# A third listed order of the recorded operations on each engine, and a third listing of the places of the rotating buffers

## The chip, the cores and the metric

The kernel runs on one core of a Trainium2 chip. That core has a matrix engine (TensorE, PE in the rows), a vector engine (VectorE, DVE), a scalar engine (ScalarE, ACT), a general engine (GpSimd, POOL), and an engine that here only issues transfers (SyncE, SP; SPq is its DMA queue). They run their own instruction lists and wait for each other through semaphores. The metric is the device time of one launch in microseconds (us).

## The reference

One layer of a hybrid decoder for 1024 tokens of width 1024, in float32: sparse attention (8 heads of 64, three gated branches) beside a state-space mixer (S5), one input and one output projection.

```python
mod = jax.nn.silu(c) @ w_ada + b_ada
shift, scale, gate = jnp.split(mod, 3, axis=-1)
h = rms_norm(x, norm_g) * (1 + scale[:, None, :]) + shift[:, None, :]
proj = h @ w_in
q, kcr, vcr, ksl, vsl, kwn, vwn, z_a, g_br, u, z_s = jnp.split(proj, offs, axis=-1)
...
attn = nsa_attention(q, kc, vc, k_slc, kv_heads(vsl), k_win, kv_heads(vwn), gates)
attn = attn * jax.nn.silu(z_a)
y = s5_mixer(u, a_re, a_im, log_dt, b_re, b_im, c_re, c_im, d_skip)
y = jax.nn.gelu(y)
y = y * jax.nn.sigmoid(y @ glu_w.astype(jnp.float32) + glu_b.astype(jnp.float32))
ssm = y.astype(x.dtype) * jax.nn.silu(z_s)
mix = jnp.concatenate([attn, ssm], axis=-1) @ w_out
return x + gate[:, None, :] * mix
```

The compressed branch works on 63 blocks of keys, the selected branch on all 16 blocks of 64 keys up to the token (with 16 blocks in all every valid one is selected), the window branch on the last 512 keys.

## The kernel before

**Recording and issuing.** Nothing is issued where the code stands. Each `Recorder` puts an operation into the list of its job and engine; a job is a named piece of the layer. Then the text `ORD` is read from left to right: `ma3:s` issues the next operation of job `ma3` on SP, `u1m:p2` the next two of job `u1m` on PE (p PE, a ACT, v DVE, g POOL, s SP; x opens or closes a pool). `in_order` ties each engine to this order, so an engine executes its list strictly in a row: an instruction that waits holds up all that stand behind it on its engine. For SP that means that a transfer that waits holds up every later transfer. All instructions are issued by `issue`, so every row of the profile names line 375; the tiles tell them apart.

**Rotating buffers.** `SLOTS` gives for each kind of buffer the place that each allocation in turn takes: `w4` has 19 places of 4 KB for each partition, `w2` 13, `f2` 6, and `S`, `mm`, `pv` are places in PSUM. A new user of a place waits for the last reader of the one before it.

**The stages**, by the times of the profile:
- 0 to 33 us: the conditioning. `sc` is silu(c) broadcast over the partitions. Each `mod_chunk` loads 512 KB of w_ada (`wada`) and reduces it on DVE against `sc` into a column of `macc`: jobs `mb0` to `mb7` give the shift of the eight blocks of 128 features, `ma0` to `ma7` the scale, `mod0` to `mod7` the gate (needed at the output). `mc` makes the columns `gs` and `sh` of a block from them. x comes in two halves of four tiles; job `sq` squares and sums, `rstd` takes the inverse root, `xsc` scales the rows (DVE and ACT two tiles each), `xb` transposes by block and half on PE (`ptr`), `h` applies `gs` and `sh` on ACT into a high and a low part (`hhi`, `hlo`).
- 33 to about 280 us: the projections. A weight block `wraw` is split into `wh` and `wsp`; three 512-column matmuls for each block and half (high by high, high by low, low by high) give `ptp` (jobs `kva`, `kvb`, `qa`, `qb`) or `pcp` (`u`, `cz`/`z`, the compressed keys). In the same time the S5 parameters and its four scans: `xload` loads `s5X` from a DRAM copy `ud`, `scan` runs on DVE over the tiles `zw` and `z`, `prep` builds the tables of the next one on POOL and DVE (`ta`, `tb`, `s5CA`).
- about 300 to 655 us: attention, in the order of token blocks 0 to 3, then 7 to 4. Job `ha`*ih* computes the scores of block *i* and head *h* (`S`, PE) and reduces and exponentiates them (`st` on DVE, `pp` on ACT), `hb` and `hs` normalize, `hc` writes the fp16 pair `hl` and has SP load it transposed (DMA_TRANSPOSE `PT<-hl`), `ub`*ih* multiplies `PT` with the values (64-column matmuls `po<-V,PT`). `at`*i* loads the finished block back (`A<-ad`) and transposes it (`pat`), `ao` is its output projection. `z` pieces, `glu` (`pglu`) and the output projection (`po<-wo,oh`) fill PE between them.
- to 665 us: the last heads, `last_out`, `last_halves` and the stores.

Of the kernel before, what the change touches and what calls it, by code (L numbers as in the profile page):

```python
# [39 lines left out]
mb7:v xb11:p3 u3m:p2 h11:a u3m:p kva3:p mc5:v kva3:p s5p:v h11:a kva3:p s5p:v2 kva3:p s5p:v mc7:v kva3:p h40:a kva3:p3  # L40
# [266 lines left out]
    sm="012034143156747476471375146",  # L307
    vtmp="01",
    pos="01",
    S=(  # L310
        "0101100110100101011010010101010101001010010100101010101010101011010010101011010101010101010100101010"
        "1101"),
    w2s="01",
# [3 lines left out]
    b="0123313020",  # L317
    a="0122320300120312031320",
# [1627 lines left out]
```

## Time and profile before

| | |
|---|---|
| median of 3 runs | 666.67 us (665.85 to 672.79) |
| the profiled execution | 666.91 us |
| its span, first to last instruction | 665.1 us, so 1.8 us lie around it |
| mean granted clock of TensorE | 0.991 |
| PE busy | 611.2 us of the span |
| DVE busy | 565.0 us |
| ACT, POOL busy | 378.1 us, 150.6 us |

Busy time of an engine is the time in which it executed something. Matmuls overlap each other, so a busy PE is not necessarily at its best rate; the starts of matmuls that follow each other in a row tell that. An idle time has a releaser, the event after which the engine went on. A number in square brackets behind a row is such an idle time in us.

### The profile page before, as it was taken

The numbers are of one execution on the slowest core, as the hardware profiler recorded it, in microseconds if no ns is written. First come the engines' busy times: TensorE is split into PE (matmuls) and PEld (weight loads), VectorE is DVE, ScalarE is ACT, GpSimd is POOL, SyncE is SP. The second block draws the span as 40 slices with busy tenths as digits, with TensorE's granted clock in tenths as the row PEclk, the third lists the DMA queues.
The fourth block names the chain that finished last, engine by engine and source line by source line (L and its number), as shares of the span: only waits on it lengthen the run. The fifth ranks groups of instructions, "written<-read, shape, count | busy, mean of one in ns | idle before, by whom it ended". The sixth has DMA issues, their size and how long they took to land.

```text
span 665.1 us, 12579 instructions
## 1 busy us (share of the span) xinstructions
PE 611.2 (92%) x4662; PEld 493.3 (74%) x4662; DVE 565.0 (85%) x1107; ACT 378.1 (57%) x732; POOL 150.6 (23%) x162
## 2 busy tenths in 40 slices
PE   2198999999989999999989999899999989999986
PEld 0186888888778887878878777556787878788865
DVE  5999999899948799796777879889989979999864
ACT  2487433745335442446767686676775856766740
POOL 0134213604952012522120110213100213011010
PEclk9998999999989999999999999999999989999999
DMA  9984223425495642526449759999798899999987
GB/s 332 382 282 122 48 64 104 147 66 137 137 272 161 191 126 49 144 80 175 123 92 237 173 112 218 231 173 236 177 199 169 176 184 209 291 219 192 228 189 178
DMA packets 209759, 116.76 MB, mean 176 GB/s; under 512 B 159073, under 2 KB 188513, under 8 KB 209698
## 3 DMA queue, kind: packets, MB, share of 16 engines
q1 hardware_dynamic: 205858, 109.38, 67.4%
q0 software_dynamic: 3840, 6.57, 4.4%
q8 instruction: 37, 0.61, 0.4%
q14 instruction: 24, 0.20, 0.1%
HBM read 58.10 MB, written 18.61 MB: 115 GB/s over the span
## 4 chain that ended last, share of the span: by engine, by line
PE 37%; DMA 7%; DVE 4%; ACT 2%; issue 1%; SPq 1%; POOL 0%; POOLq 0%; ACTq 0%; DVEq 0%
PE po L375 16%; PE pcp L375 8%; PE S L375 8%; DMA PT<-hl 4%; PE pglu L375 2%; DVE st L375 1%; SPq L375 1%; DVE hl L375 1%; DMA za<-zad 1%; DMA wor<-in_w_out_dram 1%; ACT pp L375 1%; PE pqr L375 1%; ACT hl L375 1%; DMA xo<-in_x_dram 1%; PE pc L375 1%
## 5 line engine op out<-in xcount | busy, mean ns | idle before, releaser
L375 ACT ACTIVATE pp<-S,st 128x640 f32<-128x640 f32 (+7 forms) x128 | 89.0, 698 | 51.0 <-DVE st L375 33.7
L375 ACT ACTIVATE hl<-pp,st 128x640 f16<-128x640 f32 (+7 forms) x128 | 89.0, 730 | 32.5 <-DVE st L375 14.2
L375 DVE SCALAR_TENSOR_TENSOR hl<-pp,st,hl 128x640 f16<-128x640 f32 (+7 forms) x128 | 95.8, 776 | 11.6 <-ACT hl L375 11.5
L375 DVE TENSOR_REDUCE st<-S 128x1 f32<-128x640 f32 (+7 forms) x96 | 83.7, 884 | 13.0 <-PE S L375 12.5
L375 PE MATMUL pcp<-hhi,wh 128*128 128x512 f32 x208 | 84.1, 404 | 1.4 <-ACT G L375 1.1
L375 PE MATMUL po<-wo,oh 128*128 128x512 f32 x264 | 82.9, 399 | 1.7 <-DVE ps L375 0.8
L375 PE MATMUL ptp<-wsp,hhi 128*128 128x512 f32 x256 | 83.6, 407 | 0.0
L375 PE MATMUL pcp<-hhi,wl 128*128 128x512 f32 x208 | 82.3, 395 | 0.0
L375 PE MATMUL pcp<-hlo,wh 128*128 128x512 f32 x208 | 82.2, 395 | 0.0
L375 PE MATMUL po<-V,PT 128*128 128x64 f16 x1584 | 58.9, 194 | 6.4 <-DMA PT<-hl 6.3
L375 PE MATMUL S<-kT,qh 128*128 128x128 f32 (+3 forms) x192 | 61.3, 377 | 1.1 <-ACT pp L375 0.9
L375 PEld LDWEIGHTS <-PT 128*128 128x128 f16 x1584 | 54.1, 98 | 9.0 <-DMA PT<-hl 7.2
L375 PEld LDWEIGHTS po<-wo,oh 128*128 128x128 f32 x264 | 48.8, 188 | 14.0 <-ACT oh L375 1.3
L375 PEld LDWEIGHTS ptp<-wsp,hhi 128*128 128x128 f32 x256 | 48.2, 193 | 10.7 <-ACT V L375 0.2
L375 PE MATMUL S<-kT,ql 128*128 128x128 f32 (+3 forms) x192 | 54.2, 340 | 0.0
L375 PE MATMUL ptp<-wsp,hlo 128*128 128x512 f32 x128 | 51.6, 403 | 0.0
L375 PE MATMUL po<-wo,ol 128*128 128x512 f32 x120 | 47.4, 395 | 0.6 <-POOL ol L375 0.6
L375 PEld LDWEIGHTS pcp<-hhi,wh 128*128 128x128 f32 x208 | 39.2, 189 | 10.7 <-ACT G L375 1.5
L375 POOL TENSOR_TENSOR qr<-ropeb 128x512 f32<-128x512 f32 x16 | 23.5, 1489 | 102.2 <-DVE st L375 36.1
L375 PEld LDWEIGHTS pcp<-hlo,wh 128*128 128x128 f32 x208 | 39.1, 188 | 9.2 <-issue 0.2
L375 PEld LDWEIGHTS pcp<-hhi,wl 128*128 128x128 f32 x208 | 39.2, 188 | 8.1
L375 DVE SCALAR_TENSOR_TENSOR wada<-wada,sc 128x1024 f32<-128x1024 f32 x24 | 31.2, 1312 | 10.1 <-DMA wada<-in_w_adaT_dram 10.1
(310 smaller groups left out, 1291.0 us busy)
## 6 DMA issues: line engine op xcount, KB each, us to landing
wada<-in_w_adaT_dram SPq DMA_DIRECT2D x24, 512.0 KB, 7.8
wr<-in_w_in_dram SPq DMA_DIRECT2D x14, 512.0 KB, 4.3
x<-in_x_dram SPq DMA_DIRECT2D x8, 512.0 KB, 6.4
wor<-in_w_out_dram SPq DMA_DIRECT2D x8, 512.0 KB, 6.1
out_dram<-o SPq DMA_DIRECT2D x16, 256.0 KB, 2.7
wraw<-in_w_in_dram SPq DMA_DIRECT2D x15, 256.0 KB, 5.1
xo<-in_x_dram SPq DMA_DIRECT2D x14, 256.0 KB, 3.4
ud<-U SPq DMA_DIRECT2D x4, 512.0 KB, 2.8
```

The costliest lines, as they stand in the source:

```text
L375: op(*now(a), **{n: now(x) for n, x in k.items()})
```

## The change

Two tables are exchanged: `ORD`, the order of issue, and `SLOTS`, the places of the buffers. The jobs, their operations and the number of operations of each job on each engine stay the same (6602 operations in all), as do the flags `FLG` that choose engines, the code behind them and the sizes of the tables. The order differs nearly everywhere; the diff shows the first line of each table and the places below show the order that comes of it.

```diff
 ORD = """
-pre:v xl_1:s pre:s3 s5l:s lb:s s5l:s pre:s sc0:p pre:s2 ma3:s sq0:v mb1:s sc0:a s5p:v sc0:v ma1:s sq1:a s5p:v lb:s
-sc1:p s5p:v3 ma2:s s5p:v3 mb2:s s5p:v sq2:v sc1:a ma0:s sq4:a sc1:v ma5:s sq3:v mb3:s mb1:v xl_1:s ma3:v kvaw0:s xl_1:s
...
+prep0:g kvaw0:s xl_1:s s5l:s2 pre:s3 kvaw0:a pre:s2 kvaw0:g pre:s pre:v mb2:s s5p:v ma0:s sc0:p s5p:v2 lb:s s5p:v2 lb:s
+s5p:v4 sq0:v mb0:s sc0:a s5p:v sc0:v sq1:a ma1:s s5p:v sc1:p s5p:v2 sq4:a s5p:v5 sq2:v sc1:a sq3:v ma5:s kvaw1:s sc1:v
...
     w4=(
-        "0123425678098559AB83B5C2D97BCEF56AG79HE56I081CFCBBBD7HB32GAD8GC593BCD3C9C753A2BH7I958CIGA09DH7G3B7DH"
...
+        "012345674897972A0389A4BC289C7A5D4BE0FA98GB2421H3D494I095E184HGF7CC192IH94C5GI270FH70894FEGFE570H5H01"
...
```

In the order that the engines get, the waits for other engines' semaphores change in number: ACT 214 to 232, DVE 199 to 190, PE 92 to 95, POOL 90 to 93, SP 240 to 243 separate wait instructions.

**Place 1, DVE in the first 33 us.** `wada,macc<-wada,sc` is a chunk of the conditioning, `x_72<-x_72,rstd` the scaling of two tiles of the first half of x, `sh<-macc,bada` the column after which the first block can leave ACT, `sm` rows belong to the S5 parameters. Before (six more `sm` rows of the same two kinds are left out):

```order
L375 TENSOR_SCALAR x_72<-x_72,rstd 128x1024 x2
L375 TENSOR_TENSOR sm_170<-sm_170,sm_165 128x16
L375 TENSOR_SCALAR sm_170<-sm_170 128x16
...
L375 TENSOR_SCALAR gs<-macc,mod 128x1
L375 SCALAR_TENSOR_TENSOR wada,macc<-wada,sc 128x1024
L375 TENSOR_SCALAR sh<-macc,bada 128x1
```

Now:

```order
L375 SCALAR_TENSOR_TENSOR rsq<-rstd 128x4
L375 TENSOR_SCALAR gs<-macc,mod 128x1
L375 TENSOR_TENSOR rsq<-rsq,vtmp 128x4
L375 TENSOR_SCALAR gs<-macc,mod 128x1
L375 SCALAR_TENSOR_TENSOR rstd<-rsq,rstd 128x4
L375 TENSOR_TENSOR wsp<-wraw,wsp 128x512
L375 SCALAR_TENSOR_TENSOR wada,macc<-wada,sc 128x1024
L375 TENSOR_SCALAR x_72<-x_72,rstd 128x1024 x2
L375 TENSOR_SCALAR sh<-macc,bada 128x1
L375 SCALAR_TENSOR_TENSOR wada,macc<-wada,sc 128x1024 x2
L375 TENSOR_SCALAR gs<-macc,mod 128x1
L375 SCALAR_TENSOR_TENSOR wada,macc<-wada,sc 128x1024
```

The ninth chunk, which the first `sh` behind the scaling needs, stood behind the scaling and eight small `sm` rows; now the chunks that the first block needs are all ahead of it, six chunks stand ahead of the scaling instead of eight, one `wsp` row stands there in addition, and the `sm` rows have gone to the front of the list.

**Place 2, SP around the wait for the second scan.** All are loads: `wraw` a weight block of w_in, `w1s` and `w2s` weights of the compression, `wada` the chunks `mod`, `s5X` the input of a scan, `s5T` tables copied from `Kt`, `kTd` keys written out, `gq` a small gain, `dmask` a mask. Before; the second row (`wraw`) is the one that waits for the scan's `z`:

```order
L375 DMA gq_87<-in_gains_dram 64x1
L375 DMA wraw<-in_w_in_dram 128x512
L375 DMA w2s<-in_w_v_dram 128x2x64
L375 DMA wada<-in_w_adaT_dram 128x1024
L375 DMA w1s<-in_w_k_dram 128x2x256
L375 DMA wada<-in_w_adaT_dram 128x1024
L375 DMA s5X<-ud_100 16x8x128
L375 DMA wada<-in_w_adaT_dram 128x1024
L375 DMA s5X<-ud_101 16x8x128 x3
L375 DMA w1s<-in_w_k_dram 128x2x256 x3
L375 DMA s5X<-ud_100 16x8x128
L375 DMA w1s<-in_w_k_dram 128x2x256
```

Now; the second of the three `wada` rows is the one that waits for DVE:

```order
L375 DMA dmask<-in_dmask_dram 128x256
L375 DMA s5T<-Kt 16x8x16
L375 DMA w1s<-in_w_k_dram 128x2x256
L375 DMA wraw<-in_w_in_dram 128x512
L375 DMA s5X<-ud_100 16x8x128
L375 DMA wada<-in_w_adaT_dram 128x1024
L375 DMA s5X<-ud_100 16x8x128 x2
L375 DMA wada<-in_w_adaT_dram 128x1024
L375 DMA w1s<-in_w_k_dram 128x2x256
L375 DMA wada<-in_w_adaT_dram 128x1024
L375 DMA w1s<-in_w_k_dram 128x2x256
L375 DMA s5X<-ud_100 16x8x128
```

Before, the loads of this part stood in one piece behind the waiting row. Now three s5X rows, a `w1s`, a `wraw` and a `wada` of the rows shown stand ahead of the waiting one, and further on rows of `s5T` and `kTd`, which wait for other engines, are mixed in.

**Place 3, SP around the load of head 3 of block 3.** The numbers behind the names are those of the tiles: in the order before, `PT_4512` is the transposed load of that head; in the new one it is `PT_4571`. `zz` and `zad` rows move parts of the gate path, `ad` a finished block. Before:

```order
L375 DMA zz_4442<-zsd1_112 128x512
L375 DMA_TRANSPOSE PT_4446<-hl_4264 128x16x128
L375 DMA zz_4471<-zsd3_114 128x512
L375 DMA zad_110<-zz_4276 128x1024
L375 DMA_TRANSPOSE PT_4512<-hl_4302 128x16x128
L375 DMA_TRANSPOSE PT_4526<-hl_4448 128x16x128
L375 DMA zz_4554<-zsd0_111 128x512
L375 DMA_TRANSPOSE PTc_4637<-hlc_4622 128x8x128
L375 DMA_TRANSPOSE PT_4646<-hl_4358 128x16x128
```

Now:

```order
L375 DMA_TRANSPOSE PT_4422<-hl_4280 128x16x128
L375 DMA zz_4451<-zsd1_112 128x512
L375 DMA_TRANSPOSE PT_4455<-hl_4255 128x16x128
L375 DMA_TRANSPOSE PT_4474<-hl_4445 128x16x128
L375 DMA_TRANSPOSE PT_4515<-hl_4331 128x16x128
L375 DMA_TRANSPOSE PT_4555<-hl_4429 128x16x128
L375 DMA_TRANSPOSE PT_4571<-hl_4353 128x16x128
L375 DMA_TRANSPOSE PT_4594<-hl_4551 128x16x128
L375 DMA_TRANSPOSE PT_4622<-hl_4543 128x16x128
L375 DMA_TRANSPOSE PT_4644<-hl_4613 128x16x128
```

Nine of the ten rows shown are transposed loads now; before, plain transfers stood between them. Between the load of this head and the first PE row that reads it stand 39 PE rows before (1 `pglu`, 6 of 512 columns for scores, 15 `po` among them) and 113 now (13 `pglu`, 18 for scores, 63 `po`).

## Rows read from the trace of the kernel before

**Rows 1.** The page: the first line, the busy time of each engine and, in 40 equal slices of the span (16.6 us each), the GB/s that the DMA engines moved.

```profile
span 665.1 us, 12579 instructions
...
PE 611.2 (92%) x4662; PEld 493.3 (74%) x4662; DVE 565.0 (85%) x1107; ACT 378.1 (57%) x732; POOL 150.6 (23%) x162
...
GB/s 332 382 282 122 48 64 104 147 66 137 137 272 161 191 126 49 144 80 175 123 92 237 173 112 218 231 173 236 177 199 169 176 184 209 291 219 192 228 189 178
```

**Rows 2.** Busy time of each engine in six stretches: start and end, length, busy time and (instructions) of PE, weight loads, DVE, ACT, POOL, then the granted clock, the share of the DMA engines and GB/s.

```profile
0.00:33.30 33.30, 7.00 (x15) 3.11 (x16) 24.73 (x74) 12.78 (x20) 2.12 (x6) 1.00 0.96 356
33.30:182.90 149.60, 146.40 (x738) 119.98 (x738) 141.37 (x343) 77.96 (x126) 60.99 (x63) 0.99 0.43 123
182.90:199.50 16.60, 14.30 (x104) 12.57 (x103) 8.19 (x13) 5.33 (x10) 8.93 (x15) 0.90 1.00 272
199.50:415.70 216.20, 211.28 (x1434) 173.21 (x1434) 175.76 (x358) 124.92 (x305) 38.56 (x50) 1.00 0.57 145
415.70:648.40 232.70, 221.41 (x2218) 175.57 (x2217) 207.36 (x307) 155.56 (x268) 38.71 (x29) 0.99 1.00 205
648.40:665.10 16.70, 10.80 (x162) 8.85 (x160) 7.56 (x14) 1.56 (x5) 1.27 (x1) 0.93 0.75 178
```

**Rows 3.** What PE waited for in the whole span: tile that waited, releaser, us in total, times, longest.

```profile
PE ptr L375 <- DVE x L375: 16.5, 1, 16.5
PE po L375 <- DMA PT<-hl: 6.3, 5, 2.4
...
PE pkt L375 <- DVE kh L375: 2.3, 1, 2.3
PE pat L375 <- DMA A<-ad: 2.0, 1, 2.0
```

**Rows 4.** DVE in order of time, 10 to 31 us: start, duration, operation, output<-inputs, shapes.

```profile
14.55 1.23 DVE L375 SCALAR_TENSOR_TENSOR wada<-wada,sc 128x1024 f32<-128x1024 f32 x1 [0.84 <-DMA wada<-in_w_adaT_dram]
...
15.70 1.22 DVE L375 SCALAR_TENSOR_TENSOR wada<-wada,sc 128x1024 f32<-128x1024 f32 x1
...
25.60 2.31 DVE L375 TENSOR_SCALAR x<-x,rstd 128x1024 f32<-128x1024 f32 x2
27.83 0.16 DVE L375 TENSOR_TENSOR sm<-sm,sm 128x16 f32<-128x16 f32 x1
...
29.55 1.22 DVE L375 SCALAR_TENSOR_TENSOR wada<-wada,sc 128x1024 f32<-128x1024 f32 x1
...
30.80 0.21 DVE L375 TENSOR_SCALAR sh<-macc,bada 128x1 f32<-128x1 f32 x1
```

**Rows 5.** The same stretch on ACT and PE, each in order of time (PE from 27 us).

```profile
31.11 0.78 ACT L375 ACTIVATE hhi<-ptr,sh,gs 128x512 fp32r<-128x512 f32 x1 [1.25 <-DVE vtmp L375]
...
27.30 2.20 PE L375 MATMUL ptr<-ident,x 128*128 128x128 f32 x8 [16.54 <-DVE x L375]
...
33.38 1.20 PE L375 MATMUL ptp<-wsp,hhi 128*128 128x512 f32 x2
```

**Rows 6.** Busy time in a part of the projections, columns as in rows 2.

```profile
99.70:166.20 66.50, 66.50 (x376) 55.26 (x376) 61.66 (x114) 34.27 (x54) 25.91 (x23) 1.00 0.39 113
```

**Rows 7.** The stretch around 190 us: what SP's queue waited for longest there, and the first load after that wait; DVE and PE, each in order of time; and the granted clock in the last piece of it.

```profile
SPq L375 <- DVE z L375: 12.8, 1, 12.8
...
182.65 0.33 SPq L375 DMA_DIRECT2D wraw<-in_w_in_dram  x1
...
176.43 3.25 DVE L375 TENSOR_TENSOR z<-z 64x512 f32<-64x512 f32 x2
179.72 2.90 DVE L375 TENSOR_TENSOR z<-z,zw 64x512 f32<-64x512 f32 x2
...
191.49 1.23 DVE L375 SCALAR_TENSOR_TENSOR wada<-wada,sc 128x1024 f32<-128x1024 f32 x1 [3.89 <-DMA wada<-in_w_adaT_dram]
...
191.45 1.50 PE L375 MATMUL ph<-G,w1s 128*128 128x128 f32 x12
195.25 1.11 PE L375 MATMUL pkt<-ident,kr 128*128 128x128 f32 x4 [2.30 <-DVE kh L375]
196.16 4.11 PE L375 MATMUL ph<-G,w1s 128*128 128x128 f32 x24
...
195.50:199.50 4.00, 4.00 (x23) 3.92 (x23) 3.55 (x6) 1.89 (x4) 0.00 (x0) 0.61 1.08 276
```

**Rows 8.** The z tiles of the scans on DVE (durations in ns, least, median and most), and POOL's tensor operations with kr, by group: count, busy us, mean ns of one, idle before.

```profile
L375 DVE TENSOR_TENSOR z<-z,zw x12: 684/690/1436, 138.8 to 270.5; 64x512 f32<-64x512 f32 x8, 128x512 f32<-128x512 f32 x4
...
L375 POOL TENSOR_TENSOR kr<-ropeb 128x512 f32<-128x512 f32 x8 | 13.6, 1709 | 46.3 <-DVE ropeb L375 46.3
```

**Rows 9.** Transposed loads: the landing times of all 120 of them, and the three longest waits of PE for one, each in PE's order of time.

```profile
DMA to landing us min/median/max: 2.3/3.9/8.6
...
346.38 0.35 PE L375 MATMUL po<-V,PT 128*128 128x64 f16 x6 [1.59 <-DMA PT<-hl]
...
431.65 0.58 PE L375 MATMUL po<-V,PT 128*128 128x64 f16 x14 [2.38 <-DMA PT<-hl]
...
539.70 1.10 PE L375 MATMUL po<-V,PT 128*128 128x64 f16 x21 [1.93 <-DMA PT<-hl]
```

**Rows 10.** The end, on PE in order of time: its wait for A, and the last rows of the last head's scores.

```profile
633.50 0.63 PE L375 MATMUL pat<-ident,A 128*128 128x128 f32 x4 [2.00 <-DMA A<-ad]
...
634.66 0.29 PE L375 MATMUL S<-dmask,identb 128*128 128x128 bf16 x2
```

More of the change, by code (lines that the diff above doesn't have):

```diff
@@ new lines @@
+so1:v so2:g ha76:p4 ub71:p so5:a ub71:p7 ha76:v ub71:p4 ub73:p5 qt61:a ub73:p4 ha60:p4 hc75:v hb75:a ha60:p ct7:s
+so2:p2 hb74:a so2:p2 so1:v so2:p ha76:a so2:p hc74:v so2:p2 so4:a so2:p2 hs77:v hc75:v hc75:s so2:p2 ha61:p2 hs77:v
+at0:a qt61:v ha61:p3 at0:g ha61:p ub71:p8 ha61:v ub71:p so0:s ub71:p3 ub73:p2 hb77:a ub73:p3 ub36:p3 ub73:p6 ub70:p6
+ub71:p so2:v ub71:p5 ub37:p3 ub73:p6 ub74:p2 hb76:a ub74:p3 ha60:v ub74:p hc74:s ub72:p6 ca6:p4 ha61:a hc77:v ca6:p
+so2:p3 hb76:a so2:p2 hc76:v hc75:s so2:p ha60:a so2:p4 ca6:v so2:p hc76:s so2:p hc76:v ha60:p5 ca6:v so2:v ha60:p
@@ new lines @@
+ha63:p4 ha60:v ha63:p hc77:s ub71:p6 ha60:a ub72:p ha63:v ub72:p5 ub73:p6 ub72:p3 ub74:p6 ub72:p6 hb77:a ub75:p2
+ub35:p3 ub73:p2 ca6:v ub73:p4 ub72:p6 ub34:p3 ub74:p4 ha63:a ub74:p2 ub75:p2 so0:v ub75:p4 ub73:p4 ub75:p5 hc76:s
+ub75:p ub74:p6 hs61:v ha62:p2 so4:v ha62:p3 hs61:v so4:p hb61:a so4:p ha62:v so4:s so4:p3 ca6:a so4:p2 hc61:v hb61:a
+so4:p4 hc77:v so4:p ha62:a hc61:s ca5:p4 hc61:v ha62:p3 ca5:a ha62:p2 ca6:v ha62:p ub72:p4 hc61:s ub72:p2 ub74:p6
+ub72:p ha62:v ub72:p5 ub76:p12 ub77:p6 ha64:p3 ha62:a ha64:p hc77:s ha64:p ca5:p hb60:a ca5:p ha64:v ca5:p3 ha63:p2
@@ L306 @@
[L306 to L318 removed]
+        "0111234156743869242966132578AB4AC611C79C13860513C048B5018B006BC40173A85610BA7C30B4689A82319507C6B94A"
@@ new lines @@
+    sm="012034453463111616134714536",
+    pv="00010101010100011001000111001010000010111111100000000001101000101010100010",
+    vtmp="01",
+    S=(
+        "0101101011001011010101010101010100110100101010110010101010101010101010101010101101001010101010110110"
+        "1010"),
+    mm=(
+        "0100101010101010101000110110010110010010011000101010111010010100101011010010101010010011001010101001"
+        "01011100101"),
+    w2s="01",
+    b="0122331022",
+    a="0123331021123012031230",
+    pos="01",
@@ L319 @@
     pbh="01",
     mc="01010101",
-    lc="01010101",
-    st="01210310210231023102310231023102",
-    f2="01234053533140005243145120301452313450130242023230213534052134",
+    lc="01001010",
+    st="01230123013201320132031023102310",
+    f2="01230345241232045034230543150452401425134053435453102503425130",
     p4="01231320")
```

513 lines of the change are left out of this document (249 added, 264 removed).

## The prediction

> **What bounds the kernel now.** I read the busy times of the page first [rows 1]. Matmuls fill PE for 611.2 of 665.1 us and DVE is busy for 565.0, so no third engine can set the time for long; what a new order can change is the time in which PE stands. The profiled execution took 666.91 us, 1.8 more than its span and 0.24 more than the median of the three runs, so the sum below is made against 666.91 and needs no correction for the median. Then the stages [rows 2] say where each engine has room. In the first 33.3 us PE does next to nothing (7.00 us) and DVE 24.73: this stage is a chain through DVE. From 33.3 to 182.9 PE is full (146.40 of 149.60) but DVE is busy for 141.37, so both engines hold the stage. From 182.9 to 199.5 DVE falls to 8.19 of 16.60. From 415.7 to 648.4 PE is busy for 221.41 and DVE for 207.36 of 232.70, with the DMA engines at a share of 1.00. Third, the list of PE's waits [rows 3]: 16.5 us until x is scaled at the start, 6.3 us in five waits for transposed loads, 2.3 for the keys `kh`, 2.0 for a load of A. These four are the places where an order can save something by moving one row, and I take the change at each of them, plus the stage in which DVE is the other bound. A tally of the listed order beside the measured starts shows that before the two run within half a microsecond of each other on every engine, so distances in the list can be read as time.
>
> **Start, -3.6 us.** PE's first projection matmul starts at 33.38, 2.27 after `hhi` starts on ACT at 31.11, which waited for `sh` on DVE at 30.80 [rows 4, 5]. So DVE's list up to `sh` is the path. Its chunks run back to back from 14.55 at 1.15 us each (15.70 less 14.55), and at 27.83 the `sm` rows begin that last until 29.55, when the ninth chunk starts. In the new list three chunks fewer stand ahead of `sh` (six instead of eight ahead of the scaling, none instead of one behind): 3 x 1.15 = 3.45. The `sm` rows, 29.55 - 27.83 = 1.7 less the short `gs` row that stays, count 1.5; they go to the front, where DVE waits for x anyway (their cost if that cover were missing is the same 1.5). One `wsp` row is added, about half a chunk of the same kind of row with half the columns, 0.6. One weight block of 0.25 MB is loaded ahead of x; at the 332 GB/s of the first slice [rows 1] that delays the first chunk by 0.75. Sum: -3.45 - 1.5 + 0.6 + 0.75 = -3.6. The bounds: -1.9 if DVE waits for two of the six chunks as it does for the first at 14.55 (0.84 each), and -5.9 if two of the six don't hold the scaling (2 x 1.15), because they land while DVE is at x.
>
> **33 to 183 us, +2.0.** An earlier start of PE meets a DVE that has 61.66 us of work in the 66.5 us from 99.7 on, while PE has no gap at all [rows 6]. I summed the durations of the rows of both lists up to equal amounts of PE work: between 100 and 150 us of PE work the new list asks DVE for 47 to 49 us of work where the old one asks for 42 to 43. The 5 us more stand against 4.8 us of DVE idle in the rows; not all of it can be used, since rows wait for each other. I put the loss at 2.0, nearer to full use of the idle time because the same tally has DVE's work 1 to 3 us lower from 5 to 50 and from 150 to 200. Bounds 0 and +5.0.
>
> **The stall at 190 us, -2.0.** SP waits 12.8 us for the scan's `z` and issues the next load at 182.65; then all loads of that piece come at once, DVE waits 3.89 for one of them until 191.49, PE waits 2.30 for `kh` until 195.25, and the granted clock of the next 4 us is 0.61 [rows 7]: TensorE is at its lower level, 1.2 instead of 2.4 GHz, for most of that piece, after standing still. Twelve `ph` matmuls took 1.50 before the gap and 24 took 4.11 behind it, 1.1 more than twice 1.50. So 2.3 + 1.1 = 3.4 can be had. In the new list loads of this group stand ahead of the wait and others are spread behind it; but rows of `s5T` and `kTd`, which wait for other engines, stand among them, and whatever is behind them on SP waits too. I take somewhat more than half, -2.0, with bounds 0 and -3.4.
> The same wait has a second side. Two 64-partition `z` rows took 3.25 us and two more 2.90 [rows 7], 1.4 to 1.6 each, where the median of such a row is 0.69 [rows 8]; POOL runs its table rows beside them. The new list has POOL's `kr` rows (1.71 each, [rows 8]) beside this scan and its table rows a little later, so I expect no less overlap and give it no term.
> The Trainium skill, page "SBUF — State Buffer", says in the part on its two physically separate sides that the port pair which VectorE and GpSimd share is an exclusive lock, and the loser blocks for the whole instruction of the other. The long `z` rows agree with it in kind; by that rule the scan would be as slow beside `kr` as beside the table rows, SP's wait would stay 12.8 us long, and this term would be 0 instead of -2.0, the sum 663.3.
>
> **Transposed loads, -2.0.** In the old list the load of head 3 of block 3 has 39 PE rows between it and its first reader, which add up to 4.87 us; PE waited 2.38 for it at 431.65 [rows 9]. Now it has 113 rows and 18.3 us. The wait of 1.59 at 346.38 also loses its cause (3.58 to 9.21 us in the list); the one of 1.93 at 539.70 doesn't (5.03 to 4.45). Over all heads the median distance grows from 7.14 to 8.69, against landing times of 3.9 in the median and 8.6 at most. 2.38 + 1.59 = 4.0 can go. But nine such loads now stand almost in one piece on SP, and in that stage DVE and the DMA engines have little room [rows 2], so I count half: -2.0. Bounds 0, and -4.4 (6.3 less 1.93) if every wait except the last named goes.
> The Trainium skill, page "DMA: Bandwidth & Descriptors", section "Latency and other measured facts", gives 261 GB/s for a transposed load with a split middle dimension; 512 KB at that rate are 2.0 us, an estimate. By it 4.87 us would have been enough ahead of time, nothing would be gained by the move, and the sum would be 663.3; the trace differs, its least landing time is 2.3 and the median 3.9, so here the row decides.
>
> **The end, 0.** The load of A for block 5 cost 2.00 at 633.50 [rows 10]. In the new list it has 3.63 us of PE work ahead of its reader instead of 4.15, but is the second instead of the fifth transfer behind the head that it needs: no change. The last head's scores end at 634.95 [rows 10], 30.2 before the end of the span. They stand 18.0 us of PE work before the end of the list now, 22.4 before. If the chain behind them (reduce, exponent, `hl`, transposed load, `ub`, stores) can't be compressed, that is +4.4; in the old order PE was busy with other rows nearly all the time, so the chain has room and I take 0. Bounds -2.0 and +4.4.
>
> **Sum:** 666.91 - 3.6 + 2.0 - 2.0 - 2.0 + 0 = 661.3. All lower ends give 651.2 (-15.7), all upper ends 674.4 (+7.5).
>
> **Rivals.**
> *A, DVE takes the lead back.* If DVE holds the pace until 415 us, the 3.6 of the start return as waits of PE on DVE, and the stall is only moved: 666.91 - 2.0 = 664.9. For it: 94% busy DVE up to 183 [rows 2]. Against: its 16.6 us at half load from 182.9 on, in which a late DVE could catch up.
> *B, slower: attention tiles are held too long.* In the new list the last `ub` rows of head 7 of block 0 stand at 330 us of PE work instead of 300, those of heads 37 and 70 (block, head) at 425 instead of 404. Their `PT` tiles keep a place of the 19 in `w4` that much longer. If the next user of one such place is a load that SP reaches earlier, SP stands, and every transposed load behind it. A hold of 21 us longer, less the median distance of 8.7 that covers it, is 12.3 late for PE: with the start's gain 666.91 - 3.6 + 12.3 = 675.6. It decides from a hold that outlasts the cover by 10.4 us (3.6 + 6.8); below that the time stays within 1%.
> *C, all the waits go:* start -5.9, stall -3.4, loads -4.4, DVE 0: 653.2. For it: the four places are one row each, and DVE has 100 us of idle time in the whole span.
> *D, nothing changes on balance:* each engine's order does differ, but the gains at these places come back as waits elsewhere: 666.9.
>
> **Numbers.** What a measurement of this kernel can tell from no change is about 1%, here 660.0 to 673.3. Forecast 0.40, its own range 657.5 to 664.5, half of it under 660.0; C 0.20; A 0.18; D 0.10; B 0.12. Faster by over 1%: 0.20 + 0.20 = 0.40. Within: 0.20 + 0.18 + 0.10 = 0.48. Slower: 0.12. The range that leaves out the further half of C and most of B is 652 to 670.
>
> **What would show it.** The first `ptp` matmul at 29.8 (27.5 to 31.5); no DVE idle of over 2 us and no clock under 0.9 between 180 and 200; the sum of PE's waits for `PT` under 4.5 instead of 6.3, none over 1 us at block 3 head 3; PE idle between 100 and 166 us (by the old count) of 1 to 3 us with DVE as releaser; a load wait at A of about 2. Rival A would show as PE waits for DVE between 60 and 180 us that sum to the gain of the start, B as one long wait of SP's queue for PE between 350 and 480 with PE idle behind it. I would be wrong if the many waits of under 1 us, which the order changes everywhere and for which I have no term, sum to more than these places.

## The result, and the profile after

The changed kernel took 639.95 us in the median of four runs (637.93 to 643.35), the kernel before 667.28 beside it: a ratio of 0.958, 95% interval 0.951 to 0.965. That is 27 us faster where 5.6 were forecast, and outside the range of 652 to 670. The two profiled executions took 666.91 and 643.35 us, with spans of 665.1 and 640.3; what follows compares the spans, 24.8 us apart. (The profiled execution of after is the longest of its four.)

The page of after: its first line, busy times, and the granted clock in 40 slices.

```profile
span 640.3 us, 12597 instructions
...
PE 604.2 (94%) x4662; PEld 488.4 (76%) x4662; DVE 560.2 (87%) x1107; ACT 377.6 (59%) x732; POOL 143.1 (22%) x162
...
PEclk9999999999999999999999999999999999999999
```

Against [rows 1], PE's idle time fell from 53.9 us (665.1 - 611.2) to 36.1, which is 17.8 of the 24.8. The other 7.0 are in PE's busy time: the same 4662 matmuls were busy for 604.2 instead of 611.2. The mean granted clock rose from 0.991 to 1.000. Behind three waits of before (2.15 us at 61.67, 2.30 at 195.25, 1.93 at 539.70) PE's rows ran at the lower level for a while, as in [rows 7]; by the distances between their starts this cost 1.6, 1.7 and 1.6 us, some 5 of the 7.0. So a wait can be paid twice, and the waits alone don't give the sum. It need not be: one run of the old order (the second try at the start, in experiment 4) waited as long for the same row, 2.14 at 63.16, and its clock did not fall. PE was busy for 609.3 us in that run at a mean clock of 0.998, so the clock isn't all of the difference, and the remaining 2 us of the 7.0 have no cause here. Before, and then that run (columns as in [rows 2]):

```profile
62.00:66.00 4.00, 4.00 (x14) 3.22 (x12) 3.76 (x13) 4.00 (x7) 2.16 (x3) 0.57 0.37 124
```

```profile
63.00:67.00 4.00, 3.84 (x19) 3.21 (x20) 3.69 (x15) 4.00 (x8) 1.66 (x2) 1.00 0.46 138
```

What PE waited for, as in [rows 3] (tile, releaser, us in total, times, longest):

```profile
PE ptr L375 <- DVE x L375: 12.3, 1, 12.3
PE pcb L375 <- DVE sm L375: 5.7, 1, 5.7
PE S L375 <- ACT pp L375: 2.4, 4, 0.8
PE pcb L375 <- DVE sc L375: 1.9, 1, 1.9
PE po L375 <- DVE ps L375: 1.5, 1, 1.5
...
PE po L375 <- DMA PT<-hl: 0.9, 2, 0.5
...
PE ptr L375 <- ACT hf L375: 0.7, 1, 0.7
```

The transposed loads cost 0.9 instead of 6.3; the waits for `kh` and `A` are gone; the one for `hf` is 0.7. In before it was the third longest of the list, and [rows 3] leave it out:

```profile
PE ptr L375 <- ACT hf L375: 5.3, 2, 3.1
```

Once the projections run, no wait of PE is longer than 1.5 us.

The start, rows of DVE, ACT and PE, each in order of time (answering [rows 4, 5]):

```profile
14.22 1.22 DVE L375 SCALAR_TENSOR_TENSOR wada<-wada,sc 128x1024 f32<-128x1024 f32 x1
...
23.30 1.41 DVE L375 TENSOR_SCALAR x<-x,rstd 128x1024 f32<-128x1024 f32 x2
24.62 0.20 DVE L375 TENSOR_SCALAR sh<-macc,bada 128x1 f32<-128x1 f32 x1
```

```profile
24.46 1.06 ACT L375 ACTIVATE sq<-x 128x1024 f32<-128x1024 f32 x1 [0.55 <-DMA x<-in_x_dram]
25.43 0.19 ACT L375 ACTIVATION_READ_ACCUMULATOR sq<-x 128x1 f32 x1
25.52 0.76 ACT L375 ACTIVATE hhi<-ptr,sh,gs 128x512 fp32r<-128x512 f32 x1
```

```profile
24.10 2.21 PE L375 MATMUL ptr<-ident,x 128*128 128x128 f32 x8 [12.29 <-DVE x L375]
27.00 1.12 PE L375 MATMUL ptr<-ident,x 128*128 128x128 f32 x4 [0.70 <-ACT hf L375]
27.77 1.20 PE L375 MATMUL ptp<-wsp,hhi 128*128 128x512 f32 x2
```

`sh` starts 6.18 earlier (24.62 against 30.80), `ptp` 5.61 (27.77 against 33.38): 0.6 went to ACT, where `hhi` stood behind an `sq` row.

Busy time by stage, columns as in [rows 2] (PE, weight loads, DVE, ACT, POOL, clock, DMA share, GB/s):

```profile
27.70:170.00 142.30, 142.30 (x720) 116.73 (x720) 128.75 (x344) 79.21 (x131) 46.04 (x49) 1.00 0.49 141
170.00:196.00 26.00, 24.81 (x177) 21.73 (x176) 22.01 (x32) 7.14 (x13) 20.36 (x30) 1.00 0.74 207
```

PE has no gap from its first projection to 170 us, and the clock holds through the stretch where it was 0.61 before [rows 7].

**Where the time went.** To compare stretches of two orders I counted PE's work: each matmul stands for the usual distance from its start to the next one's for its kind, and the table gives the time at which so much work had been started. All kernels but after and before are experiments (below); "measured places" are a new listing for the same order.

```
us of PE work:                6     31    106    156    231    306    331    406    506    581
before                     34.7   65.3  142.3  199.6  278.2  363.0  389.0  472.4  586.3  659.6
after                      29.1   55.9  132.8  185.5  262.7  345.2  372.3  452.9  563.7  634.8
new start, then old        29.1   55.2  135.7  190.7  269.6  355.3  381.8  465.0  576.7  650.2
new two thirds, then old   28.5   55.6  132.4  184.7  261.6  343.7  376.8  459.1  572.3  645.2
old two thirds, then new   34.6   65.1  142.0  196.9  276.7  362.5  389.1  468.6  579.0  649.8
old order, measured places 35.1   64.6  142.8  196.9  273.2  355.4  381.7  461.5  575.1  647.1
new order, measured places 28.6   56.0  132.8  184.4  261.5  343.4  369.3  447.4  565.6  635.6
```

After leads by 5.6 us at 6 us of work, 9.4 at 31, 9.5 at 106, 14.1 at 156, 17.8 at 306 and 24.8 at the end. Some 70% of it is there half way through, and from 31 to 106, where both engines are full, nothing of it is lost. By the size of the loss (a matmul's start later than its usual distance): losses of over 1 us fell from 19.0 us at 11 places to 5.0 at 4; those of 0.3 to 1 us stayed (8.8, 9.1); those of 0.1 to 0.3 fell from 10.8 to 5.5.

### The profile page after: what moved, and what is told of

It reads as the page before. It is cut to its first block, busy times and chain, and to the rows that moved or that the text cites. A ratio compares the mean times of both kernels' runs of the same rounds, so it can differ in the third digit from the quotient of the medians.

```text
span 640.3 us, 12597 instructions
## 1 busy us (share of the span) xinstructions
PE 604.2 (94%) x4662; PEld 488.4 (76%) x4662; DVE 560.2 (87%) x1107; ACT 377.6 (59%) x732; POOL 143.1 (22%) x162
## 4 chain that ended last, share of the span: by engine, by line
PE 26%; DVE 11%; DMA 10%; issue 4%; ACT 3%; POOL 1%; SPq 0%; ACTq 0%; DVEq 0%; POOLq 0%
PE po L375 12%; PE S L375 6%; DMA PT<-hl 6%; PE pcp L375 5%; DVE hl L375 4%; DVE st L375 3%; DVE ps L375 1%; ACT pp L375 1%; DMA wor<-in_w_out_dram 1%; ACT hl L375 1%; DMA wr<-in_w_in_dram 1%; DMA yd<-Y 1%; DMA zz<-zsd 1%; PE pc L375 1%; POOL qr L375 1%
## 5 line engine op out<-in xcount | busy, mean ns | idle before, releaser
L375 ACT ACTIVATE hl<-pp,st 128x640 f16<-128x640 f32 (+7 forms) x128 | 90.0, 732 | 28.8 <-DVE st L375 13.1
L375 DVE SCALAR_TENSOR_TENSOR hl<-pp,st,hl 128x640 f16<-128x640 f32 (+7 forms) x128 | 97.6, 783 | 5.1 <-ACT hl L375 4.8
L375 POOL TENSOR_TENSOR qr<-ropeb 128x512 f32<-128x512 f32 x16 | 21.8, 1381 | 96.3 <-DVE ropeb L375 56.1
L375 PEld LDWEIGHTS S<-kT,qh 128*128 128x128 f32 x192 | 33.2, 190 | 8.1 <-ACT pp L375 3.0
```

The costliest lines, as they stand in the source:

```text
L375: op(*now(a), **{n: now(x) for n, x in k.items()})
```

## The experiments

Three questions are open, and the expectations name their theories by them. Does an early lead survive, or does DVE take it back behind the stretch that made it? Are the waits single rows, which a single move can take away, or does each stretch go as its whole list goes? And how much is the order, how much the listing of places? A mixed kernel takes the first entries of one list (an entry is one operation of a job) and then the rest in the other's order. Its places are a question of their own, since each listing belongs to one order.

**1. Mixed orders that keep both listings.** The places of both parts were renamed so that each allocation has its own listing's place, with 4, 6 and 0 of them changed at the joint. The last tokens ahead of the joint and the first behind it:

```diff
 ORD = """
-pre:v xl_1:s pre:s3 s5l:s lb:s
+prep0:g kvaw0:s xl_1:s s5l:s2 pre:s3 kvaw0:a pre:s2 kvaw0:g
...
+u1:p s5p:v2 u1:p s5p:v kvb3:p s5p:v cmpv:s pre:g hidk:s cKC:s
```

> The new order up to 50 us of PE work, the old one behind it, with both listings of places kept: those of the old one are renamed at the joint, so that only 4 allocations take another place. If a lead is kept: 9.5 less than before, 657. If the DVE work that the new start has put off (5.5 us) has to be paid in the full stage behind the joint: 660 to 663. If the lead is taken back: 665.

New order for 579 entries (about 50 us of PE work), then the old: **657.63 us, ratio 0.982 (0.977 to 0.987).** The lead is 10.1 at 31 us of work, 6.6 at 106, and 8.9, 8.6, 7.2, 9.4 at 156, 231, 331 and 581. Of the 3.5 lost up to 106, 0.9 go at the joint (a wait of 0.71 at 78.76), and 2.5 some 30 us later, in full stretch, where PE meets rows of POOL and DVE that come too late for it:

```profile
109.76 0.66 PE L389 MATMUL pkt<-ident,kr 128*128 128x128 f32 x4 [0.91 <-POOL kr L389]
...
111.12 0.26 PE L389 MATMUL pk<-s5c,BD 128*48 128x16 f32 x2 [0.29 <-POOL BD L389]
...
113.54 0.66 PE L389 MATMUL pkt<-ident,kr 128*128 128x128 f32 x4 [0.81 <-DVE kh L389]
```

Neither before nor after has a wait of PE between 31 and 106 us of work. So the old list takes a quarter of the lead back there. The 2.3 that return up to 156 are the stall at 190 us, which was shorter in this run; behind it the old order neither takes the lead back nor adds to it. Its rest shows the old waits in the old places, earlier by the lead ([rows 9, 10] had 2.38 at 431.65 and 2.00 at 633.50). PE, waits in order of time:

```profile
425.12 0.58 PE L389 MATMUL po<-V,PT 128*128 128x64 f16 x14 [2.54 <-DMA PT<-hl]
...
624.85 0.63 PE L389 MATMUL pat<-ident,A 128*128 128x128 f32 x4 [2.61 <-DMA A<-ad]
```

> The same joint at 304 us of PE work (342.7 us of time in the new kernel, 360.5 in the old): new order up to there, old one behind, 6 allocations on another place. If the stages add up and the listings are what broke the earlier mixed kernels: 17.8 less than before, 649. If attention in the old order does not bear an earlier start: over 655.

New order up to about 304 us of PE work (2934 entries; joint at `z5_5:p z5_3:p ub00:p3`): **655.21, ratio 0.979 (0.973 to 0.984).** It follows after to 306 (19.3 ahead of before), loses 7 just behind the joint in two waits for `PT` (2.14 at 348.06, 1.34 at 355.19) and what they delay, and goes like the old order from there.

> The counterpart at 322 us of PE work (379.5 us of time): old order up to there, new one behind, every allocation on the place that its listing gives, renamed. If the stages add up: 24.8 - 18.1 = 6.7 less than before, 660. If the new second half is quick only behind the new first half: 665 or more.

Old order for 3194 entries, then the new: **657.68, ratio 0.981 (0.976 to 0.987).** At 331 us of work it is level with before (389.1 against 389.0), and behind it gains 9.8, without the waits at block 3 head 3, at block 6 head 4 and at A. (On the way it was 2.7 ahead at 156, since its stall at 190 us was shorter: the wait for `kh` was 1.61, with no fall of the clock behind it. That much one execution differs from another at this place.) So the new front, with its listing, is worth some 17 to 19 us and the new last part, with its listing, some 7 to 10. The gain is spread over the program.

**2. Places alone.** The order is kept, and `SLOTS` is written anew by a rule. "Plain": the free place whose last reader stands furthest back in the list. "Measured": the place whose last reader ended first by the trace of that order. The first characters of `w4` (old order, measured rule):

```diff
     w4=(
-        "0123425678098559AB83B5C2D97BCEF56AG79HE56I081CFCBBBD7HB32GAD8G
+        "0123456789ABCDEFGHI2609BD31578ACHE09FG631I8CH7A27D57D920G5EB72
```

> The new order whole, but its listing of buffer places replaced by a plain rule: each allocation takes the place whose last reader stands furthest back in the list. If the order alone makes the gain: within 0.5% of the new kernel, 638 to 643. If the listing of places matters: over 645.

New order, plain places: **663.89, ratio 0.994 (0.991 to 0.998)**: 24 us of the 27 are lost by places alone. By after's measured times 37 of its allocations fall due before their place is released, by 51.8 us in all. It runs like after up to 156 us of work, then come waits such as these on PE, which after doesn't have:

```profile
208.43 6.21 PE L391 MATMUL ph<-G,w1s 128*128 128x128 f32 x36 [4.99 <-issue]
...
528.11 1.08 PE L391 MATMUL pqr<-ident,qr 128*128 128x128 f32 x4 [8.25 <-DVE ps L391]
```

> The old order whole, with the plain rule for the places that cost the new order 24 us (the place whose last reader stands furthest back in the list). By the times of the trace of before, 26 allocations then meet a place that is not yet free, 29.8 us in all, against 37 and 51.8 us for the new order. If the old listing of places is worth as much for its order as the new one for its own: 675 to 685. If the old listing is no better than the plain rule, so that the new listing is what makes the gain: 660 to 670.

Old order, plain places (26 such allocations, 29.8 us): **669.35, ratio 1.000 (0.997 to 1.003)**, no worse than its own listing.

> The old order, its places dealt out anew by the measured times of the trace of before: each allocation takes, of the places that are free in the list, the one whose last reader ended first by the trace (950 of 1210 allocations fall on another place; two would meet a place that is not free, 0.8 us in all). If the old order was held up by its listing: 655 or less. If the old order sets its own time and any listing without conflicts gives it: 662 to 669.

Old order, measured rule (950 of 1210 allocations in another place): **656.46, ratio 0.984 (0.979 to 0.989)**, so 11 us without moving one instruction. The start is as before; the gain begins with the stall at 190 us. SP's wait for the scan's `z` was 12.8 us long [rows 7]; here SP's queue waits

```profile
SPq L390 <- DVE z L390: 3.7, 1, 3.7
```

the weight block is issued at 172.12 instead of 182.65, PE's wait for `kh` doesn't occur, and the 20 us from 180 on, where before had PE busy for 17.70 at a clock of 0.91, are full (PE first, then weight loads, DVE, ACT, POOL, clock):

```profile
184.00:188.00 4.00, 4.00 (x30) 3.64 (x28) 0.00 (x0) 1.09 (x2) 3.92 (x6) 1.00 0.81 200
188.00:192.00 4.00, 4.00 (x41) 3.11 (x40) 3.58 (x6) 1.08 (x3) 3.88 (x9) 1.00 1.07 350
192.00:196.00 4.00, 4.00 (x33) 3.80 (x32) 2.63 (x5) 2.89 (x7) 1.44 (x3) 1.00 0.87 178
```

PE is busy 604.9 us in this kernel, like after. The load had waited for its place, not for its turn: in two runs that keep the old listing up to there (the old two thirds of experiment 1, the four moves of experiment 4) the queue waits for `z` for 12.1 and 11.6 us, and with plain places for 4.5. The three waits of [rows 9] (1.59, 2.38, 1.93) are gone, 1.50 and 1.41 here.

> The new order with the same rule by the measured times of its own trace (928 allocations on another place, one conflict of 0.6 us planned). If the 24 us that the plain places cost came from allocations that met a place not yet free: 638 to 645. If the listing does something else for the time: 655 or more.

New order, measured rule (928 changed): **640.18, ratio 0.958 (0.954 to 0.963)**, like after, although its profiled execution has one wait of 5.13 for a transposed load at 508.39.

```
median us          plain   own listing   measured rule
old order          669.4         667.3           656.5
new order          663.9         640.0           640.2
```

Read along the rows, the old listing cost the old order 11 us, and the new listing costs the new order nothing that this rule can find. Read down, the order is worth 16 us when both have measured places, and 5.5 with plain ones (3.4 by the two ratios, since the two ran beside different runs of before): the order's gain needs places that follow it.

The table of PE's work says where each of the two acts. From 156 to 581 us of work before takes 460.0 us, after 449.3, the old order with measured places 450.2 and the new order with them 451.2. So 9.8 of the 10.7 us that after gains behind the stall are also had in the old order, by places alone. Ahead of it the order acts: with measured places in both, the new order leads by 6.5 us at 6 us of work, 10.0 at 106 and 12.5 at 156, and by 11.5 at the end. (These are the profiled executions, 11.6 us apart; the medians are 16.3 apart, so a few us may lie behind 156 in others. The new order's has the wait of 5.13.)

**3. Mixed orders with other places.** These came first, and were meant to answer the first question. The joint of the first, and the first characters of its `w4`:

```diff
 ORD = """
...
+kvb3:p s5p:v2 kvb3:p s5p:v cmpv:s pre:g hidk:s cKC:s u3m:p3
...
     w4=(
+        "012345674897972A0389A4BC289C7A5D4BE0FA98GB2421H3DI049045E897C1
```

> The new order up to 50 us of PE work (552 entries of the list, about 75 us of time in the new kernel), then what is left in the old order; places of the buffers as in the table of each part where free. Theory L (a wait that is removed is worth its length where it stands, and nothing takes it back): the new kernel is 9.4 us ahead at this point, so about 657.5. Theory R (the new order keeps DVE's work back: at 50 us of PE work it has asked DVE for 5.5 us less than the old one, and that reserve is what lets the lead pass the stage where DVE is the bound): the old rest has to do those 5.5 us first, so 660 to 663. Theory G, the step of the prediction that DVE takes the lead back whatever the order: 664 to 667.

> The new order up to 190 us of PE work (behind the stall at 190 us of time), then the rest in the old order. L and R agree: 14.2 us ahead at this point, and DVE has room behind it, so about 652.7. G: above 660.

> The counterpart: the old order up to 190 us of PE work, then the rest in the new order. If the gains of the two parts add up: 25 - 14.2 = 10.6 us less than before, about 656.3. If the second half's gain hangs on the first half's lead (attention starting earlier, so that loads are ready), 660 or more.

With the old place where free, otherwise the one free longest: new start (552 entries) **679.58, 1.016 (1.008 to 1.023)**; new to 190 us of PE work **664.79, 0.996 (0.993 to 0.999)**; old to 190, then new **676.21, 1.015 (1.012 to 1.018)**. In the first a lead of 9.3 is there at 31 us of work, the joint takes 4.4, and 4.5 to 9.4 are kept to 306; then 6.4, 6.4 and 8.4 us are lost to before in three stretches of 25 us of work in the attention, where PE waits for the last reader of a score buffer's place:

```profile
520.77 0.22 PE L389 MATMUL S<-dmask,identb 128*128 128x128 bf16 x1 [3.42 <-ACT pp L389]
...
603.51 1.01 PE L389 MATMUL S<-kT,qh 128*128 128x128 f32 x2 [3.82 <-ACT pp L389]
```

The second lost 9.1 at its joint (`pk` waited 6.37 for a `zw` on ACT) and shows the old waits behind it (1.41, 2.43, 2.13 at the three rows).

> As the first of these mixed kernels (new order up to 50 us of PE work, old order behind it), but the places are dealt out by measured times: each allocation takes, of the places that are free by the traces of the two kernels, the one released last before it is needed; by these times no allocation waits. L (removed waits are kept): 9.4 us less than before, 657.5. R (the new order has held back 5.5 us of DVE work at this point, which the old rest has to do in the stage where DVE is full): PE loses 3 to 5.5 us between 80 and 110 us of time, 660 to 663, and no more behind it. G (DVE takes the lead back): 665 or more, with the loss spread over the time up to 183 us.

> The new order up to 226 us of PE work (all projections of the first 260 us), then the old order; places by measured times (two allocations of all wait, 1.8 us together). L and R: the new kernel is 15.4 us ahead there, so about 651. If the time of the old second half depends on when it starts: over 656.

> The old order up to 226 us of PE work, then the new one; places by measured times, no allocation waits. If the two halves add up: 24.8 - 15.4 = 9.4 less than before, about 657.5. If the second half's gain needs the lead of the first: 662 or more.

Places by measured times, but the one released last ahead of the need ("best fit"), with the joints at 50, 226 and 226 us of PE work: **680.4, 1.018 (1.015 to 1.022)**; **682.66, 1.021 (1.018 to 1.024)**; **675.56, 1.011 (1.008 to 1.013)**. By the planned times no place was late in the first of these, and all three are slower than before. The first of them and the new start of experiment 1 have nearly the same order (552 and 579 entries from the new list) and are 22.8 us apart. So a listing isn't good because every place is free in time by the plan. That a place released long ago stays free when something is late, and one released just ahead of the need doesn't, is my reading; no run tests it by itself, and the first three kernels, which took the place free longest only where the old one was taken, were slow as well.

**4. Single moves in the old order,** own listing. The diff by entries (job and engine): the start, a column of block 6, head 3 of block 3, and the load of A:

```diff
-sq3:v mb3:s
+sq3:v mb0:s
...
-mc2:v rstd0:v mb3:v
+mc2:v rstd0:v mb0:v
...
+xsc0:v mc0:v
...
-xb70:p s5p:v xb70:p2 s5p:v mc6:v
+xb70:p mc6:v s5p:v xb70:p2 s5p:v
...
-ub33:p6
...
+glu11:p ub33:p12
...
+hc43:s at5:s
...
-ao71:p ao10:v ao71:p2 at5:s
```

> The old order and its own listing of places (one allocation falls on another place), with four single rows or groups moved: in the start the chunks mb0 and mb3 change places on SP and DVE and the sh column of block 0 follows the scaling of x; the sh column of block 6 stands ahead of an S5 row that took 3.27 us on DVE beside POOL work; the first twelve rows of head 3 of block 3 stand behind the next pglu piece on PE; the load of A for block 5 stands behind the next transposed load instead of five transfers later. If each wait is worth its length and is kept: first ptp matmul 2.7 earlier (30.7 instead of 33.38), no wait at 61.7 (2.15), none at 431.7 (2.38), none at 633.5 (2.00): 9.2 in all, 657.5. If DVE takes the lead back in the stage up to 183 us: the first two (4.9) are gone by then, 662.5. If the next place in the line waits instead everywhere: 665 or more.

**667.04, ratio 0.998 (0.995 to 1.002).** Each of the four moves did its part and gave it back. `sh` came 2.98 earlier, at 27.82, but ACT had two `sq` rows ahead of the `hhi` that waits for it, and `ptp` came only 0.33 earlier, at 33.05:

```profile
28.58 1.04 ACT L390 ACTIVATE sq<-x 128x1024 f32<-128x1024 f32 x1
...
30.80 0.76 ACT L390 ACTIVATE hhi<-ptr,sh,gs 128x512 fp32r<-128x512 f32 x1
```

The other three waits were replaced by waits of the next in line: one at 61.67 for `hf` (2.15 before), the one at 431.65 and the one at 633.50 became

```profile
62.90 0.50 PE L390 MATMUL pu<-hlo,wh 128*128 128x512 f32 x1 [2.35 <-DMA hlo<-hf]
...
432.66 0.26 PE L390 MATMUL S<-dmask,identb 128*128 128x128 bf16 x1 [3.05 <-ACT pp L390]
...
636.87 0.66 PE L390 MATMUL pat<-ident,A 128*128 128x128 f32 x4 [1.44 <-DVE za L390]
```

The second try took the start alone and put the two rows of block 0 ahead of `sq` on ACT too:

```diff
-kvaw1:s s5p:v3 sq6:a kvaw3:s s5p:v xb10:p xb00:p2 s5p:v xb00:p
+kvaw1:s s5p:v3 kvaw3:s s5p:v xb10:p xb00:p2 s5p:v xb00:p h00:a2 sq6:a
```

> The old order with the start alone changed: mb0 and mb3 exchanged and the sh column of block 0 behind the scaling of x, as in the kernel with four moves, and also on ACT the two rows that make hhi and hf of block 0 ahead of the two sq rows of the second half of x, which stood in front of them and ended at 30.8 there. If ACT's list was the next to be late: hhi starts at about 28.6 instead of 31.1, the first ptp matmul at 30.9 instead of 33.4, and by what the mixed kernels showed (a lead of the start is kept) about 664.5. If nothing comes of it, another engine is late next: 666 to 668.

**669.04, ratio 1.001 (0.998 to 1.004).** `ptp` came at 32.54, 0.84 earlier, since `hhi` now waited for PE's transposes (the scaling ended on ACT at 29.07), and by 31 us of work the lead was gone in further waits for `wsp` and `x` on DVE.

```profile
26.88 2.19 ACT L390 ACTIVATE x<-x,rstd 128x1024 f32<-128x1024 f32 x2 [1.50 <-DVE rstd L390]
30.27 0.78 ACT L390 ACTIVATE hhi<-ptr,sh,gs 128x512 fp32r<-128x512 f32 x1 [1.21 <-PE ptr L390]
```

**5. A try at a faster kernel:** the new order with POOL's first `wsp` row behind `sc`, and ACT's `sq` behind the two rows of block 0.

```diff
-pre:s3 kvaw0:a pre:s2 kvaw0:g
+pre:s3 kvaw0:a pre:s2
...
+sc0:v kvaw0:g
...
-xb00:p2 sq5:a xb10:p4
+xb00:p2 xb10:p4
...
-h00:a kvaw4:s
+h00:a sq5:a kvaw4:s
```

> The new kernel with two rows moved in its start: POOL's first wsp row, for which DVE's ones waited until 5.5 us, goes behind the first sc row of DVE, and ACT's sq5 behind the hhi and hf rows of block 0. DVE is busy from 5.5 us on until the first hhi, so up to 1.9 us from the first (the old kernel's pcb started at 3.82, the new one's at 5.74) and up to 0.9 from the second; if a lead of the start is kept, 637 to 639 where the new kernel has 640; no change if DVE's first S5 rows wait for their data.

**639.21, ratio 0.956 (0.952 to 0.960)**, no different from after; its first `ptp` stands at 27.85, not earlier.

## Why the prediction was wrong

The direction held, and the sum missed 19.2 us of the gain. Two steps failed, with 15.8 of these between them: the loss of 2.0 that I put on DVE between 33 and 183 us, where 5.1 were gained, and the 2.0 for all that lies behind the stall, where 10.7 were gained. In the spans the terms compare so (us):

| term | forecast | measured |
|---|---|---|
| start, to the first `ptp` | -3.6 | -5.6 |
| from there to the stall (6 to 131 us of PE work) | +2.0 | -5.1 |
| the stall (131 to 156) | -2.0 | -3.4 |
| all behind it: transposed loads -2.0, the end 0 | -2.0 | -10.7 |
| sum | -5.6 | -24.8 |

**Start.** The path was right, down to `hhi`. In the forecast, chunks, `sm` and `wsp` came to -4.35; measured they are -4.94 (from the first chunk to the scaling 9.08 instead of 11.05, and 2.97 from the scaling to `sh` gone altogether). The 0.75 for the extra load ahead of x was wrong: the first chunk came 0.33 earlier. The scaling took 0.91 less, which the trace of before could have told me (last section), and ACT's `sq` gave 0.59 back. Together -5.6, in the bounds.

**33 to 183 us, the step with the wrong sign.** I read two busy engines and an increment: 5 us more work for DVE between 100 and 150. The same tally, taken as a running sum, has DVE's work behind the old order's by 5.5 us at 50 us of PE work, 7.9 at 100 and 2.9 at 156: DVE comes to the dense stretch with a reserve. The traces agree. Up to the point where 234 matmuls have run (50 us of PE work), DVE was busy for 73.20 us in before and 64.55 in after (columns as in [rows 2]):

```profile
0.00:84.40 84.40, 55.95 (x234) 42.76 (x235) 73.20 (x225) 46.25 (x69) 19.81 (x23) 0.98 0.71 234
```

```profile
0.00:74.90 74.90, 54.24 (x234) 41.64 (x235) 64.55 (x201) 46.99 (x70) 17.38 (x20) 1.00 0.77 262
```

Measured, the stretch from 31 to 106 costs the same in both (77.0 and 76.9), so the lead passes through whole. With the old list behind the new start, which has to make up what DVE had put off, 2.5 of 10.1 us went in that stretch: the place that theory R of the expectations named, and about half of its 5.5. **Rival A is refuted as I put it** (all of the start's gain back, and DVE setting the pace to 415 us), in the new order and in the mixed one; that the reserve is what spares the new order the loss is made likely by this, not shown.

The rest of the -5.1 is gain I had no term for: -3.8 from 6 to 31 us of work. One wait accounts for it, the one at 61.67: 2.3, and 1.6 more for the rows behind it at the lower clock. It is one of the two waits for `hf`, 5.3 us in all, that I had left out when I took four waits for all that an order can save. Its cause is a row of DVE that a row of POOL held (last section). The rest, 1.2 from 106 to 131, is PE's wait of 1.05 for `G` on ACT at 169.07, which after doesn't have. PE in before, in order of time:

```profile
61.67 0.74 PE L375 MATMUL ptr<-ident,x 128*128 128x128 f32 x4 [2.15 <-ACT hf L375]
...
169.07 0.50 PE L375 MATMUL pcp<-hhi,wh 128*128 128x512 f32 x1 [1.05 <-ACT G L375]
```

**The stall.** The size came near (3.4 was the upper end), by luck: the cause was wrong, and the old two thirds of experiment 1, with the same front, lost only 1.0 to after in this piece. I took it that loads stand behind a waiting one in SP's list, and that moving them ahead gains. The old order with other places has no stall: the load waited for its place in `w2`. Whether that one place alone would do wasn't tried.

**Transposed loads and the end, the step that missed most.** I looked for the price of this part in the order, and most of it was in the places: 9.8 of its 10.7 us come in the old order too when only the places change (experiment 2). The prediction asked of no load there whether it waited for its place. The list distance was a poor predictor. Block 6 head 4's wait was to stay (5.03 to 4.45 us in the list) and went; A's load, with less work ahead of it than before, no longer waits. Experiment 1 shows that these waits come with the old order and its listing (the new ones behind the old two thirds have none at block 3 head 3 and A), and experiment 4 that a single move trades one for another. Places alone do the same: the old order with plain places waits 0.9 us in all for `PT` and not at A, but 13.1 for `pp`. My sum priced the four visible waits as if nothing stood behind them and as if the rest were at its floor. The losses of under 1 us, which I had named as what would make me wrong, gave 5.0 of the 19.3 that PE lost less behind its start (5.3 from those of 0.1 to 0.3); the places of over 1 us gave 14.0.

**The listing.** The prediction gave it no term, only rival B (a tile held too long, slower). That mechanism is real, and worth 24 us in the new order with plain places, but it had been costing the kernel before: 11 us, which no term of the sum held. Of the rivals C, "all the waits go", came nearest in kind; its 653.2 was too high because its sum holds only the waits that I had listed.

**What I said would show it.** The first `ptp` between 27.5 and 31.5: it is at 27.77. Clock of no less than 0.9 from 180 to 200: 1.00. No DVE idle of over 2 us there: there is one of 3.06 at 182.76, without any cost to PE. `PT` waits under 4.5: 0.9. PE idle of 1 to 3 us with DVE as releaser: none. A wait of about 2 at A: none.

**What stays open.** Order and places can't be parted cleanly, because a listing is made for an order; 16 and 11 us is the split by one rule. Which of the 950 places hold up the old order behind the stall wasn't traced. Why the new two thirds lose 7 us just behind the joint, with only 6 places changed, was seen (two transposed loads, late) but not traced to its root.

## What to carry to other kernels

An order and the places of its buffers are one thing: before moving an instruction that waits, see whether it waits for its data, its turn or its place, and when writing a listing take the place that has been free longest by the measured times, not merely one that is free; for both orders here that rule was the best or level with the best. Deal the places out anew for the old order first: here this gave 11 us without a move. Where two engines are both nearly full, compare their work as running sums from the start, not by the increment of one stretch. A wait that ends a chain is worth only its distance to the next late engine in the same list: price several moves together, and test them by joining the head of one order to the tail of another, with each part's places kept.

## What the runs showed of the hardware

In these traces a row of DVE beside POOL's work can last until POOL's row is over, and so cost far more than its own work. In before, DVE and POOL in order of time:

```profile
56.34 3.27 DVE L375 TENSOR_TENSOR sm<-sm,sm 128x32 f32<-128x32 f32 x1
```

```profile
56.70 1.61 POOL L375 TENSOR_TENSOR hlo<-hf,hhi 128x512 fp32r<-128x512 f32 x1
57.95 1.60 POOL L375 TENSOR_TENSOR wsp<-wraw,wsp 128x512 fp32r<-128x512 f32 x1
```

Rows of this `sm` kind take 0.19 a little later (60.09, 60.53). This one ended at 59.61, 0.06 behind the second POOL row. In seven other runs of the old order the row took 3.25 to 3.27 too. It delayed the `sh` of block 6, then ACT's `hf`, then PE: the wait of 2.15 at 61.67. The Trainium skill, page "SBUF — State Buffer", in the part on its two physically separate sides, calls the port pair that the two engines share an exclusive lock; the row agrees in kind, though it was held over two POOL rows in turn.

The scaling of x shows the same. Its two rows took 2.31 in before, where POOL's `wsp` ran from 25.43 to 26.70 beside them, and 1.41 in after. In seven other runs of the old order they took 1.40, but there a small row ahead of them met POOL's and took 1.10 to 1.21 instead of 0.16, so that the time was paid all the same. In the run with four moves, DVE and then POOL:

```profile
25.29 1.11 DVE L390 SCALAR_TENSOR_TENSOR rstd<-rsq,rstd 128x4 f32<-128x4 f32 x1
...
26.50 1.40 DVE L390 TENSOR_SCALAR x<-x,rstd 128x1024 f32<-128x1024 f32 x2
```

```profile
25.07 1.30 POOL L390 TENSOR_TENSOR wsp<-wraw,wsp 128x512 fp32r<-128x512 f32 x1 [24.64 <-ACT wsp L390]
```

The scaling ended at 27.90 in this run and at 27.91 in before. That overlap was 0.9 us of the start, and no view of idle times shows it: DVE counts as busy.
